# A two-layer hybrid diffusion step on one core: adaLN rows turned behind all sums, prompt tokens two k-tiles at a time, own buffers for the prompt's rotary results, last weights split later

## The chip, the cores and the metric

The kernel runs on one core of one Trainium2 chip. The metric is the device time of one launch in microseconds (us); where several runs were made, their median. Engines are named as in the profile: PE is TensorE's matmul queue and PEld its weight loads, DVE is VectorE, ACT is ScalarE, POOL is GpSimd, SP is SyncE, which issues nearly all DMAs of this kernel. Each engine works through its own queue strictly in order, so an instruction that waits holds up everything behind it on that engine.

## The reference

One step of a hybrid diffusion transformer with D = 1024 and two layers, over 1024 latent tokens ("sample") and 256 prompt tokens. Layer 0 has two head groups, a windowed attention with 16 heads and a bidirectional mLSTM with 4 heads; layer 1 is multi-head latent attention (MLA, 16 heads). Cut to what the change touches:

```python
def _adaln(cond, w, b):
    m = jax.nn.silu(cond) @ w + b                       # shift, scale, gate: 3 x 1024 columns
    shift, scale, gate = jnp.split(m[:, None, :], 3, axis=-1)
...
for l in range(DEPTH):
    sh_p, sc_p, gt_p = _adaln(c_ctx[None, :], w_mod[l], b_mod[l])
    sh_s, sc_s, gt_s = _adaln(c, w_mod[l], b_mod[l])
    hp = _rmsnorm(yp, norm_g[l]) * (1.0 + sc_p) + sh_p
    hs = _rmsnorm(ys, norm_g[l]) * (1.0 + sc_s) + sh_s
    ...                                                 # the mixer of the layer
    yp = yp + gt_p * out_p
    ys = ys + gt_s * out_s

def _mlstm_chunkwise(q, k, v, li, lf, C0, n0, m0):      # per head, chunk by chunk
    b = jnp.cumsum(lfc, axis=-1)                        # forget gates summed
    m_new = jnp.maximum(b_last + m, jnp.max(log_w, axis=-1))   # a running maximum
    w_s = jnp.exp(log_w - m_new[..., None])             # weights of the tokens
    ...

def _mixer_c(h, w_in, q_norm, w_qb, kv_norm, w_kvb, w_out, ctx, pos):
    qa, kva, kr, z = jnp.split(h @ w_in, C_SPLITS, axis=-1)
    q = (_rmsnorm(qa, q_norm) @ w_qb).reshape(B, T, C_HEADS, C_NOPE + C_ROPE)
    q_nope, q_rope = q[..., :C_NOPE], q[..., C_NOPE:]
    c_kv = _rmsnorm(kva, kv_norm)
    if ctx is not None:                                 # latent tokens only: rotary positions
        q_rope = _axial_rope(q_rope, rows, cols)
    k = jnp.concatenate([k_nope, jnp.broadcast_to(keys_kr, ...)], axis=-1)
    attn = _blocked_attn(qf, k, v, None, (C_NOPE + C_ROPE) ** -0.5)
    out = (attn * jax.nn.silu(z)) @ w_out
```

All is float32. The outputs are both token sets after the last norm, and the new caches and states.

## The kernel before, in words

**Products.** Each float32 product is three matmuls: a matrix is split into a rounded high part and the low rest, and high·high, high·low and low·high are summed in PSUM. A split is two instructions: ACT casts the high part (names that end in `h`: `wh`, `h1Th`, `cph`), then DVE or POOL subtracts it (`wl`, `h1Tl`, `cpl`). Tokens lie in three chunks, `CHUNKS`: 512 and 512 latent tokens and the 256 of the prompt.

**Order.** A first stage is written out by hand. Then comes a stage in which a scheduler puts the instructions of every engine in order (projections of layer 0, the mLSTM gates, the adaLN sums); a long hand-ordered middle (mLSTM and windowed attention); and again a scheduled rest: out projection, norm, layer 1's projections, latents and rotary parts, the MLA in seven `pair` stages with other work as filling, the output weights and the output. The scheduler keeps data dependences and orders by its own estimates, so one edit can shift the order of instructions far from it.

**PSUM.** In the first scheduled stage the 8 banks of PSUM are 6 for products (`S`) and 2 for transposes (`T`, from `psT`). A transpose writes a bank, and the bank is free once DVE or ACT has read it.

**adaLN sums** (`mod_sums`, lines 497 to 557). For six blocks of 512 columns, eight weight tiles `mw` (8 buffers) are loaded and summed by matmuls with the conditioning as stationary operand; ACT halves the sum into a tile `mrow1` (L512, `columns`). For scale and shift of layer 1 the tile must be turned to one column per token feature: `turned` transposes it on PE into a `T` bank, and DVE adds the bias (L522) and for scales multiplies by the norm's gain (L524). `mod_sums` is a generator, eight steps a block; a block's `turned` runs in the third step of the next one.

**The mLSTM's gates** (`gates`). Gate rows of 36 x 1280 are transposed in (`GI`, `GF`), scanned on DVE (L1579, L1580, L1586), combined (L1608 `LF`, L1609 `LI`, L1617 `rst`), exponentiated by ACT, and three of them go back by ten 36-row transposes each: `LI` into `cv`, `rst` into `cws`, `gM` into `cem`, each through one `T` bank that DVE copies out (L1642). `weave` alternates the steps of `gates` with shares of the projections of other blocks. DVE also has the mLSTM's convolution in its queue at that time (L1680, L1681, L1687, waiting for ACT's L1683).

**Layer 1's input** (`hT_chunk`, L785 and L786). Per k-tile of 128 features: transposes into a `T` bank, DVE scales and shifts into `hT_t`, ACT casts `h1Th`, DVE or POOL subtracts `h1Tl`. With the prompt a tile is 128 x 256.

**Rotary parts** (`k_rope`, `q_rope`, `rope_out`, `split_to`). The rotary part of keys and queries is split and stored to DRAM. The prompt's part has no rotation but goes through the same two-buffer tiles, `so_h` (ACT's cast, L867) and `rp_t` (the subtraction, L868); a buffer is free once its store has been read out by the DMA.

**Output weights** (`weights_out`, L2250 the cast `w`). Sixteen half tiles of `w_out` are loaded and each is split some steps behind its load, while the last MLA pair runs; `late` holds splits not yet issued, at most one between steps 6 and 11. In a pair, ACT also casts the transposed probabilities (`cph`, L2548), which PE needs for `V`.

## Time and profile before

| | us |
|---|---|
| median of 3 runs | 2566.37 (2564.22 to 2566.87) |
| the profiled execution | 2561.93 |
| its span in the profile | 2560.1 |
| PE busy in it | 2515.9 |
| DVE, ACT, POOL busy | 1699.3, 1437.2, 1128.9 |

The profile is one execution. Its own time is 1.8 us above its span. A row of the timeline gives the start, the length, engine and line, operation, tile out<-in, the shapes, and in square brackets how long the engine had been idle just before and what it waited for. A row of the windows gives the window, its length, busy time and number of instructions of PE, PEld, DVE, ACT and POOL, then the clock granted to PE as a share of full speed, the DMA share and GB/s. Lines are those of the kernel before; the end of a matmul is modelled, and neighbouring matmuls overlap, so that the distance of two starts, and not a row's length, is what one costs.

### The profile page before, as it was taken

The page shows a single profiled execution, that of the slowest core. Times are in us where ns is not written, and L with a number is a line of the kernel's source. Part 1 is how long each engine was busy: PE and PEld are TensorE (multiplying, and loading weights), DVE is VectorE, ACT ScalarE, POOL GpSimd, SP SyncE. Part 2 cuts the span into 40 slices and gives each one's busy share as a digit, 9 for nine tenths or more (in the row PEclk, how much of TensorE's full clock was granted, in tenths as well). Part 3 has the DMA queues.
Part 4 walks back from the last instruction along what each step waited for, and adds up shares of the span by engine and source line. Part 5 has one row for each costly group of instructions (what it writes and reads, how often), then busy time and mean ns, then how long its engine had stood idle before and what let it go on. Part 6 is the DMA issues. An engine that isn't in the chain of part 4 may idle for free.

```text
span 2560.1 us, 48511 instructions
## 1 busy us (share of the span) xinstructions
PE 2515.9 (98%) x16354; PEld 2246.2 (88%) x16354; DVE 1699.3 (66%) x4004; ACT 1437.2 (56%) x3665; POOL 1128.9 (44%) x1512
## 2 busy tenths in 40 slices
PE   8999999999999999999999999999999999999998
PEld 6998998998998888878888777898899989999887
DVE  6643656756657575687777456436888888888754
ACT  6423534535534432577666433134888888888842
POOL 6222333333324344366555543145455545555832
PEclk9999999999999999999999999999999999999999
DMA  7665575566667564455443554433211101111334
GB/s 265 214 178 177 156 222 184 170 202 190 188 205 222 181 216 151 118 171 164 128 133 94 173 159 162 124 82 114 63 35 30 39 29 41 32 31 29 123 98 134
DMA packets 339098, 347.52 MB, mean 136 GB/s; under 512 B 36425, under 2 KB 281854, under 8 KB 338594
## 3 DMA queue, kind: packets, MB, share of 16 engines
q1 hardware_dynamic: 338850, 344.43, 44.0%
q8 instruction: 130, 2.13, 0.3%
q14 instruction: 118, 0.97, 0.1%
HBM read 233.82 MB, written 110.50 MB: 134 GB/s over the span
## 4 chain that ended last, share of the span: by engine, by line
PE 83%; DVE 3%; issue 2%; ACT 2%; DMA 2%; POOL 1%; SPq 1%; POOLq 0%; DVEq 0%; ACTq 0%
PE mm L120 34%; PE S L120 28%; PE V L120 8%; PE T L124 7%; PE mm L124 2%; PE D L120 2%; SPq L155 1%; PE T L120 1%; DMA y<-w 0%; POOL w L1117 0%; DMA att_q<-ql 0%; DMA o_a<-aT 0%; ACT att_ph L1394 0%; DVE att_pl L1395 0%; POOL att_p L1383 0%
## 5 line engine op out<-in xcount | busy, mean ns | idle before, releaser
L583 POOL TENSOR_TENSOR wl<-wf,wh 128x256 fp32r<-128x256 f32 (+2 forms) x272 | 222.5, 843 | 484.3 <-ACT wh L582 396.4
L120 PE MATMUL mm<-hTh,wh 128*128 128x512 f32 (+1 forms) x912 | 329.2, 361 | 0.9 <-DVE scr L868 0.9
L120 PE MATMUL mm<-hTh,wl 128*128 128x512 f32 (+1 forms) x912 | 324.7, 356 | 0.0
L120 PE MATMUL mm<-hTl,wh 128*128 128x512 f32 (+1 forms) x912 | 324.1, 355 | 0.0
L120 PE MATMUL S<-cK,cQ 96*128 96x512 f32 (+3 forms) x1248 | 297.4, 363 | 0.8 <-ACT cPa L2501 0.7
L2549 DVE TENSOR_TENSOR cpl<-T,cph 128x512 fp32r<-128x512 f32 x336 | 228.7, 685 | 44.9 <-ACT cph L2548 41.7
L120 PEld LDWEIGHTS S<-cK,cQ 96*128 96x128 f32 (+1 forms) x1248 | 193.1, 189 | 22.3 <-ACT cPa L2501 2.7
L2548 ACT CAST cph<-T 128x512 fp32r<-128x512 f32 x336 | 192.4, 590 | 30.4 <-PE T L124 21.4
L120 PEld LDWEIGHTS mm<-hTh,wl 128*128 128x128 f32 x912 | 171.4, 188 | 26.9
L120 PEld LDWEIGHTS mm<-hTh,wh 128*128 128x128 f32 x912 | 171.5, 188 | 23.5 <-DVE scr L868 1.1
L120 PEld LDWEIGHTS mm<-hTl,wh 128*128 128x128 f32 x912 | 171.7, 188 | 23.2
L2499 DVE TENSOR_REDUCE cmx<-S 128x1 f32<-128x512 f32 x256 | 173.1, 682 | 18.2 <-PE S L120 17.1
L1395 DVE TENSOR_TENSOR att_pl<-mm,att_ph 128x512 fp32r<-128x512 f32 x168 | 116.0, 690 | 46.2 <-ACT att_ph L1394 44.0
L2480 POOL TENSOR_SCALAR cPa<-cPa,cst 128x512 f32<-128x512 f32 x128 | 98.4, 769 | 108.9 <-DVE cst L2477 92.0
L1394 ACT CAST att_ph<-mm 128x512 fp32r<-128x512 f32 x168 | 97.9, 582 | 76.0 <-PE mm L124 74.2
L120 PE MATMUL mm<-wh,hTh 128*128 128x256 f32 x480 | 135.5, 282 | 0.0
L120 PE MATMUL mm<-wl,hTh 128*128 128x256 f32 x480 | 134.9, 281 | 0.0
L120 PE MATMUL mm<-wh,hTl 128*128 128x256 f32 x480 | 134.5, 280 | 0.0
L582 ACT CAST wh<-wf 128x256 fp32r<-128x256 f32 (+2 forms) x272 | 96.4, 409 | 60.9 <-DMA wf<-in_w_in_c 28.8
L1383 POOL TENSOR_SCALAR att_p<-att_p,att_den 128x640 f32<-128x640 f32 (+1 forms) x128 | 97.5, 775 | 74.1 <-DVE att_p L1364 43.4
L1375 ACT ACTIVATE att_p<-att_p,att_nm 128x641 f32<-128x641 f32 (+1 forms) x128 | 103.4, 808 | 42.3 <-DVE att_nm L1369 35.4
L120 PE MATMUL V<-cph,cV 128*128 128x256 f32 x440 | 117.8, 288 | 1.3 <-ACT cph L2548 1.3
(489 smaller groups left out, 7908.7 us busy)
## 6 DMA issues: line engine op xcount, KB each, us to landing
wf<-in_w_in_ab SPq DMA_DIRECT2D x120, 256.0 KB
in<-in SPq DMA_DIRECT2D x40, 514.0 KB
in<-in SPq DMA_DIRECT2D x32, 386.0 KB
mw<-in_w_mod SPq DMA_DIRECT2D x48, 256.0 KB
in<-scr SPq DMA_DIRECT2D x40, 258.0 KB
o_x<-y SPq DMA_DIRECT2D x20, 512.0 KB
xin<-in_k_wmod SPq DMA_DIRECT2D x16, 512.0 KB
in<-cx SPq DMA_DIRECT2D x32, 256.0 KB
```

The lines of the kernel that those rows point to most:

```text
L120: return self.nc.tensor.matmul(out, lhsT, rhs, start=start, stop=stop)
L124: self.nc.tensor.transpose(out, in_, self.ident[:p, :p])
L582: K.nc.scalar.copy(wh, wf[:, k])
L583: K.nc.gpsimd.tensor_sub(wl, wf[:, k], wh.bitcast(F32))
L1375: self.A.K.nc.scalar.activation(pv, pv, AF.Exp, bias=nm[:, i], scale=-1.0, accum_out=den[:, i])
L1383: nc.gpsimd.tensor_scalar(pv, pv, den[:, i:i + 1], 1.0, ALU.mult, ALU.mult)
L1394: K.nc.scalar.copy(ph, self.T)
L1395: K.nc.vector.tensor_sub(pl, self.T, ph.bitcast(F32))
L2480: nc.gpsimd.tensor_scalar(pv, pv, wt[:, c:c + 1], rd, ALU.mult, ALU.mult)
L2499: nc.vector.tensor_reduce(mx[:, b, c:c + 1], S, AX.X, ALU.max, negate=True)
L2548: nc.scalar.copy(ph, T_)
L2549: nc.vector.tensor_sub(pl, T_, ph.bitcast(F32))
```

## The change

Five edits:

1. `mod_sums`: the halved sums stay in SBUF (`mrow1` gets 4 buffers instead of 2) in a list `waiting`; all four are transposed together into one `T` bank after the last sum, and the adds (after the change L524, L526) follow there.
2. `gates` has one more `yield`, before `cws`, and is woven in 6 steps instead of 5: `LI` goes out one step, `rst` and `gM` another.
3. `hT_chunk`: for the prompt a step takes two k-tiles of 256 columns in one bank; cast and subtraction work on 512 columns. Four casts and four subtractions instead of eight of each; which ones are on POOL changes with it.
4. `rope_out`: the prompt's rotary results get a pool `cu3` of their own with five buffers each for the high and the low part (`pr_h`, `pr_l`) in place of `so_h` and `rp_t`; the subtraction is on DVE. `k_rope` of the second latent chunk moves its additions from POOL to DVE.
5. `weights_out`: at most three pending splits in steps 6 to 12, one in step 13, instead of one in steps 6 to 11.

```diff
     def columns(ps, f):
-        rows = K.t(p, [128, 128], F32, "mrow1", 2)
+        rows = K.t(p, [128, 128], F32, "mrow1", 4)
         nc.scalar.mul(rows, ps[:, 0:128], 0.5)
-        return partial(turned, rows, f)
+        waiting.append((rows, f))
-    def turned(rows, f):
+    def turned():
         pc = K.psT()
-        K.tr(pc[:, 0:128], rows)
...
+        for i, (rows, f) in enumerate(waiting):
+            K.tr(pc[:, i * 128:(i + 1) * 128], rows)
+        for i, (rows, f) in enumerate(waiting):
...
+            nc.vector.tensor_add(dst, src, bc(bcol, 8 * a))
+            if a:
+                nc.vector.tensor_mul(dst, dst, bc(K.gcol, 8))
...
-            if i == 2 and late:
-                late = late()
...
-    if late:
-        late()
+    turned()
...
-    weave(gates(K, gp, gtp, gt), 5, dense.stream(2, 0.8), 20)
+    weave(gates(K, gp, gtp, gt), 6, dense.stream(2, 0.8), 20)
...
     for nm, src in (("cv", v), ("cws", ws), ("cem", M)):
         col = pp.tile([128, NT, 36], F32, tag=nm, name=nm)
+        if nm == "cws":
+            yield
         ps = K.psT()
...
-    for k in range(KD):
+    n = 512 // N
+    for j in range(KD // n):
+        ks = slice(j * n, (j + 1) * n)
...
+        hh, hl = [h[ci][:, ks].rearrange("p k t -> p (k t)") for h in (K.hTh, K.hTl)]
+        nc.scalar.copy(hh, t)
+        (nc.gpsimd if (j % 3 == 2 if n == 1 else j % 2) else nc.vector).tensor_sub(hl, t, hh.bitcast(F32))
...
+    elif not K.cu3:
+        split_to(K, K.cu2, ps, P, N, None, dh, dl, l=K.t(K.cu2, [128, 512], F32, "rp_t", 2))
     else:
-        split_to(K, K.cu2, ps, P, N, None, dh, dl, l=K.t(K.cu2, [128, 512], F32, "rp_t", 2))
+        h, l = [K.t(K.cu3, [128, 256], F32R, n, 5)[0:P, 0:N] for n in ("pr_h", "pr_l")]
+        K.nc.scalar.copy(h, ps[0:P, 0:N])
+        K.nc.vector.tensor_sub(l, ps[0:P, 0:N], h.bitcast(F32))
+        K.dma(dh, h)
+        K.dma(dl, l)
...
-            while len(late) > (1 if 6 <= i < 12 else 0):
+            while len(late) > (3 if 6 <= i < 13 else 1 if i == 13 else 0):
```

**On PE, in the stage of the gates.** Before (`mrow` tiles are turned in single transposes further up; `S<-wh,hTh` are projection matmuls):

```order
L120 MATMUL S_1931<-wh_1479,hTh_126 128x256
L120 MATMUL S_1931<-wl_1480,hTh_126 128x256
L120 MATMUL S_1931<-wh_1479,hTl_127 128x256
L124 MATMUL T_2130<-ident,LI 128x36 x10
L124 MATMUL T_2143<-ident,rst 128x36 x10
L120 MATMUL S_1956<-wh_1467,hTh_128 128x256
```

After:

```order
L120 MATMUL S_2010<-wh_1461,hTl_129 128x256
L124 MATMUL T_2044<-ident,LI 128x36 x10
L120 MATMUL S_1900<-wh_1467,hTh_126 128x256
...
L120 MATMUL S_1950<-wl_1480,hTh_128 128x256
L120 MATMUL S_1950<-wh_1479,hTl_129 128x256
L124 MATMUL T_2171<-ident,rst 128x36 x10
L124 MATMUL T_2184<-ident,gM 128x36 x10
L120 MATMUL S_2010<-wh_1467,hTh_128 128x256
```

`LI` stood directly ahead of `rst`, at place 850 of PE's queue; it now stands at place 799, with 72 projection matmuls between it and `rst`, which has moved from place 851 to 872; `gM` follows `rst` at once (before, it had 22 matmuls ahead of it, at place 874).

**On DVE, in the same stage**, between the scans and the additions that make `LI`. Before:

```order
L1586 SCALAR_TENSOR_TENSOR gM<-LF,m_1731,LI 4x1024 x2
L1664 COPY scr_1689<-S_1696 128x1
L1681 SCALAR_TENSOR_TENSOR cx_1808<-scr_1689,cw,cx_1808 128x512
L522 TENSOR_TENSOR B_1141<-T_1791,bcol_242_1137 128x4x2
L1680 SCALAR_TENSOR_TENSOR cx_1817<-scr_1804,cw,cx_1817 128x512
L1579 SCALAR_TENSOR_TENSOR gB<-rst,LF 4x1280
...
L1586 SCALAR_TENSOR_TENSOR gM<-LF,LI 4x256 x2
L1681 SCALAR_TENSOR_TENSOR cx_1817<-scr_1804,cw,cx_1817 128x512
L1687 SCALAR_TENSOR_TENSOR cx_1808<-scr_1812,cx_1808 128x512
```

After:

```order
L1590 SCALAR_TENSOR_TENSOR gM<-LF,m_1711,LI 4x1024 x2
L1583 SCALAR_TENSOR_TENSOR gB<-rst,LF 4x1280
L1584 SCALAR_TENSOR_TENSOR gB<-rst,LF 4x1280
L1590 SCALAR_TENSOR_TENSOR gM<-LF,LI 4x256 x2
L1670 COPY scr_1686<-S_1765 128x1
L1603 COPY bl<-gB 4x10
L1686 SCALAR_TENSOR_TENSOR cx_1811<-scr_1798,cw,cx_1811 128x512
L1604 COPY bl<-gB 4x10
```

The scans now follow one another; two L1681 and one L1687 of the convolution stand behind the additions that make `LI` (after the change they are L1687 and L1693), and the adaLN add L522 has left the stage.

**On PE, where the MLA begins**: behind the key transposes of the prompt (`u`), the query products `mm<-cq` of pair 0 and the key products `S<-hh`. Before:

```order
L120 MATMUL S_22448<-hh_4659_22058,wkl_22318 128x512
L124 MATMUL T_22341<-ident,u_22198 128x128
L124 MATMUL T_22336<-ident,u_22257 128x128
L124 MATMUL T_22341<-ident,u_22257 128x128
L120 MATMUL mm_22778<-cq_20199,wqh_22313 128x512
L120 MATMUL mm_22778<-cq_20200,wqh_22313 128x512
```

After:

```order
L120 MATMUL S_22433<-hh_4648_22039,wkl_22299 128x512
L124 MATMUL T_22325<-ident,u_22179 128x128
L124 MATMUL T_22320<-ident,u_22238 128x128
L124 MATMUL T_22325<-ident,u_22238 128x128
L120 MATMUL S_22444<-hh_4648_22039,wkh_22298 128x512
...
L120 MATMUL S_22500<-wvh_22302,hl_4649_22040 128x256
L120 MATMUL mm_22763<-cq_20180,wqh_22294 128x512
```

The first `mm<-cq` has moved from directly behind the transposes to 48 instructions behind them; key and value products stand there now.

**On ACT, beside the last pair**, the casts of the output weights (`w`) among the casts `cph`. Before:

```order
L2474 ACTIVATE cst_31792<-cmx_31661,cst_31792 128x3
L2250 CAST w_31695<-w_31693 128x512
L2250 CAST w_31695<-w_31720 128x512
L2548 CAST cph_31649<-T_31644 128x512
L2548 CAST cph_31675<-T_31670 128x512
...
L2548 CAST cph_31710<-T_31705 128x512
L2250 CAST w_31757<-w_31755 128x512
```

After (the same lines are L2489, L2265 and L2563):

```order
L2489 ACTIVATE cst_31773<-cmx_31646,cst_31773 128x3
L2265 CAST w_31680<-w_31678 128x512
L2265 CAST w_31680<-w_31705 128x512
L2563 CAST cph_31634<-T_31629 128x512
L2563 CAST cph_31660<-T_31655 128x512
...
L2563 CAST cph_31695<-T_31690 128x512
L2265 CAST w_31742<-w_31740 128x512
```

The first two casts stand between the same instructions as before.

## The prediction

> **What bounds the kernel now.** I read the page's head first, then the waits of PE, then the windows around the stages that the change touches.

> ```profile
> span 2560.1 us, 48511 instructions
> PE 2515.9 (98%) x16354; PEld 2246.2 (88%) x16354; DVE 1699.3 (66%) x4004; ACT 1437.2 (56%) x3665; POOL 1128.9 (44%) x1512
> PE 83%; DVE 3%; issue 2%; ACT 2%; DMA 2%; POOL 1%; SPq 1%; POOLq 0%; DVEq 0%; ACTq 0%
> ```

> PE is busy for 98% of the span, and the chain that ended last runs 83% through it. No other engine is near. The change leaves the number of matmul rows alone, so it can gain only in two ways: out of the 44.2 us in which PE stood idle (2560.1 − 2515.9), or where PE ran at a lower clock. The waits of PE say where idle time lies that the edits can reach:

> ```profile
> PE T L124 <- DVE A L522: 2.7, 1, 2.7
> PE mm L120 <- DVE rp_t L868: 2.4, 1, 2.4
> PE V L120 <- ACT cph L2548: 1.3, 1, 1.3
> PE S L120 <- ACT h1Th L785: 0.3, 1, 0.3
> PE S L120 <- POOL h1Tl L786: 0.3, 1, 0.3
> PE S L120 <- DVE sz_th L893: 0.3, 1, 0.3
> ```

> Each row is total, times, longest. These six, 7.3 us together, belong to edits 1 and 2, 4, 5 and 3 in this order. The first has a second price, which the windows show (length, then busy of PE, PEld, DVE, ACT, POOL, then PE's granted clock):

> ```profile
> 147.50:150.20 2.70, 0.01 (x1) 0.01 (x1) 1.58 (x9) 2.18 (x5) 0.00 (x0) 0.90 0.97 222
> 150.20:151.40 1.20, 1.18 (x11) 1.13 (x11) 0.84 (x5) 0.65 (x2) 0.00 (x0) 0.50 0.89 205
> 151.40:154.00 2.60, 2.60 (x13) 2.60 (x13) 1.75 (x7) 0.37 (x1) 0.00 (x0) 0.50 0.99 357
> 154.00:157.00 3.00, 3.00 (x22) 2.78 (x21) 0.00 (x0) 0.00 (x0) 0.00 (x0) 0.59 0.45 153
> ```

> After the gap PE is granted half its clock until nearly 157.

> **Edits 1 and 2, the gates.** The rows of PE and DVE around the gap:

> ```profile
> 146.70 0.81 PE L124 MATMUL T<-ident,LI 36*128 36x36 f32 x10
> 150.22 1.25 PE L124 MATMUL T<-ident,rst 36*128 36x36 f32 x10 [2.71 <-DVE A L522]
> 147.88 1.27 ACT L1618 ACTIVATE rst<-rst 36x1280 f32<-36x1280 f32 x1
> 149.49 0.42 DVE L1687 SCALAR_TENSOR_TENSOR cx<-scr,cx 128x256 f32<-128x256 f32 x1 [1.09 <-ACT scr L1683]
> 149.91 0.16 DVE L522 TENSOR_TENSOR A<-T,bcol 128x8 f32<-128x8 f32 x1
> ```

> The transposes of `rst` need a `T` bank. `LI` holds one; the other holds an adaLN row that L522 must read, and L522 is queued on DVE behind a convolution step that itself waits 1.09 for ACT. The data alone, `rst` exponentiated at 147.88 + 1.27 = 149.15, would have been late too, so both halves are needed: edit 1 takes the bank away from the adaLN row, edit 2 parts `LI` from `rst`. To price this I need the cost of a projection matmul and DVE's road to `LI`:

> ```profile
> 140.11 0.28 PE L120 MATMUL S<-wh,hTl 128*128 128x256 f32 x1
> 142.93 0.28 PE L120 MATMUL S<-wh,hTl 128*128 128x256 f32 x1
> 122.10 4.70 DVE L1586 TENSOR_TENSOR_SCAN gM<-LF,m,LI 4x1024 f32<-4x1024 f32 x2 [1.00 <-ACT LF L1567]
> 127.03 0.85 DVE L1681 SCALAR_TENSOR_TENSOR cx<-scr,cw,cx 128x512 f32<-128x512 f32 x1
> 137.70 1.04 DVE L1681 SCALAR_TENSOR_TENSOR cx<-scr,cw,cx 128x512 f32<-128x512 f32 x1
> 138.67 1.23 DVE L1687 SCALAR_TENSOR_TENSOR cx<-scr,cx 128x512 f32<-128x512 f32 x1
> 142.00 1.48 DVE L1609 TENSOR_TENSOR LI<-LI,gB 36x1280 f32<-36x1280 f32 x1
> ```

> The first two rows are 24 matmuls apart: (142.93 − 140.11) / 24 = 0.1175 us each.

> When `LI` is wanted: 51 places earlier, about 51 × 0.1175 = 6.0, so at 146.70 − 6.0 = 140.7. When it is ready: before at 142.00 + 1.48 = 143.48; two L1681, one L1687 and an L522 leave the road, 0.85 + 1.04 + 1.23 + 0.16 = 3.28, so 140.2, and up to the 1.00 that the scan waited for its input can go as well, since its transposes stand earlier too: 139.2 to 140.2. The slack is 0.5 to 1.5, thin. When `rst` is wanted: 140.7 + 0.8 for `LI` + 72 × 0.1175 = 8.5, thus 150.0. When it is ready: its road behind `LI` was 149.15 − 143.48 = 5.67; of the three operations pushed behind `LI`, 3.12, all may fall into it: 140.2 + 5.67 + 3.12 = 149.0. The slack is 1.0. The `LI` bank is needed for `gM` at 150.8, and its copy stands behind the last convolution step, whose end before was 149.49 + 0.42 = 149.9 and which has lost none of the work ahead of it but L522: slack 0.9.

> So I take the gap as gone, 2.7, and with it the low clock: 1.20 × 0.50 + 2.60 × 0.50 + 3.00 × 0.41 = 3.1. Together **5.8**. The bound above adds 2.70 × 0.10 = 0.3 for the 0.90 of the first window: 6.1. For the bound below, the thin slacks may each turn into a wait, the dearest being 1.0 at `LI`, and a queue on SP is passed:

> ```profile
> 153.05 0.32 SPq L155 DMA_DIRECT2D w0row<-dl  x1
> 156.92 0.80 SPq L155 DMA_DIRECT2D w0b<-w0row  x2
> ```

> `w0b` waits for `w0row` to land, 156.92 − 153.05 = 3.9 behind it. Two weight tiles `mw` of the next adaLN sum now stand behind `w0b`, and PE, running 5.8 ahead, reaches that sum sooner. I put nothing for it, and at most 1.5, less than half that row distance. Below: 5.8 − 1.0 − 1.5 = 3.3.

> [...]

> The added `yield` moves no data. The four transposes at the end of the sums replace four single ones, and the adds on DVE are the same six; the columns are read only by layer 1's input, over 1,300 us later, so lateness there costs nothing.

> **Edit 3, the prompt's 512 columns.** The forms of the tile (min, median, max ns):

> ```profile
> L782 DVE TENSOR_SCALAR hT_t<-T,A,B x24: 534/802/811, 1510.8 to 1579.7; 128x512 f32<-128x512 f32 x16, 128x256 f32<-128x256 f32 x8
> L785 ACT CAST h1Th<-hT_t x24: 405/620/626, 1511.7 to 1580.3; 128x512 fp32r<-128x512 f32 x16, 128x256 fp32r<-128x256 f32 x8
> L786 DVE TENSOR_TENSOR h1Tl<-hT_t,h1Th x18: 424/680/987, 1513.8 to 1580.7; 128x512 fp32r<-128x512 f32 x12, 128x256 fp32r<-128x256 f32 x6
> L786 POOL TENSOR_TENSOR h1Tl<-hT_t,h1Th x6: 722/1288/1300, 1516.5 to 1578.8; 128x512 fp32r<-128x512 f32 x4, 128x256 fp32r<-128x256 f32 x2
> ```

> The minimum is the 256 form, the median the 512 form. DVE: 6 × 0.42 = 2.5 of subtractions become 2 × 0.68 = 1.4, since two of four go to POOL; ACT: 8 × 0.405 = 3.2 become 4 × 0.62 = 2.5. DVE, which was the busy one here, gets 1.1 back, and the three waits of 0.3 (one each on ACT, POOL and DVE) hang on that supply. Against it, the last pair's subtraction is now one of 1.29 on POOL where the last one was 0.42 on DVE, 0.87 later. I take **0.7** of the 0.9; above 0.9, below 0.9 − 0.87 − 0.4 ≈ −0.4, if the last subtraction is waited for in full and a cast of 0.62 instead of 0.405 comes on top twice.

> **Edit 4, the rotary buffers.** Where the 2.4 lies:

> ```profile
> 1778.97 0.71 PE L120 MATMUL mm<-cq,wqh 128*128 128x512 f32 x2 [2.43 <-DVE rp_t L868]
> 1780.04 0.68 ACT L867 CAST so_h<-S 128x256 fp32r<-128x256 f32 x2 [1.12 <-DMA ckr<-so_h]
> 1782.25 0.84 ACT L867 CAST so_h<-S 128x256 fp32r<-128x256 f32 x2 [1.52 <-DMA cqr<-so_h]
> 1776.00:1779.00 3.00, 0.57 (x5) 0.31 (x3) 1.92 (x5) 2.65 (x6) 2.70 (x3) 1.00 0.54 185
> ```

> ACT waits 1.12 and 1.52 for stores to free `so_h`, and PE 2.43 for the banks behind these splits. With five buffers each these waits of ACT go, POOL (2.70 of 3.00 busy) loses the subtraction, and PE has 48 key and value products to do before the first `mm<-cq`. I take the whole **2.4**. That is also the bound above. Below: 1.3, if what ACT no longer waits for at 1780.04 is all that counts (1.12, and 0.2). This gap left the clock at 1.00, so it has no second price.

> **Edit 5, the weights.**

> ```profile
> 2384.00:2400.00 16.00, 14.08 (x93) 11.98 (x93) 11.82 (x28) 13.88 (x36) 14.18 (x19) 1.00 0.86 271
> 2387.35 0.62 ACT L2250 CAST w<-w 128x512 fp32r<-128x512 f32 x1 [1.02 <-DMA w<-in_w_out_c]
> 2388.73 0.62 ACT L2250 CAST w<-w 128x512 fp32r<-128x512 f32 x1 [0.76 <-DMA w<-in_w_out_c]
> 2389.25 1.06 ACT L2548 CAST cph<-T 128x512 fp32r<-128x512 f32 x2
> ```

> PE's 1.3 for `cph` is ACT's 1.02 + 0.76 on two loads with the `cph` casts queued behind. If the casts stood later, 1.92 of PE's idle here (16.00 − 14.08) could go. But in the changed order these two casts stand between the same instructions, and some of the following ones come earlier; only loads are issued further ahead. So **0**; above 1.9, below −1.2, two more casts (0.62 each) ahead of `cph` while ACT is 87% busy.

> **The rest.** The scheduler also reshuffles the MLA pairs:

> ```profile
> 1808.00:2384.00 576.00, 573.16 (x3999) 524.41 (x3998) 497.84 (x1155) 492.77 (x1364) 313.28 (x543) 1.00 0.12 35
> ```

> Only 2.84 of 576 are idle; **0**, ±1.5 (half of it).

> **Sum.** 5.8 + 0.7 + 2.4 + 0 + 0 = 8.9. On the profiled execution 2561.93 − 8.9 = 2553.0; that execution is 4.4 below the median of the runs, so for the median 2566.37 − 8.9 = **2557.5**. All upper bounds give 6.1 + 0.9 + 2.4 + 1.9 + 1.5 = 12.8, thus 2553.6; all lower ones 3.3 − 0.4 + 1.3 − 1.2 − 1.5 = 1.5, thus 2564.9.

> **Rivals.**

> *The weights do gain.* The loads, issued further ahead, have landed when the two casts come, and 1.9 is added: 2555.6. For it: 1.02 and 0.76 are waits for loads. Against it: the DMA share is 0.86 in that window, and the first two loads are no earlier.

> *The clock is lost anyway.* `LI` comes late by 1.0, the ten small transposes and that gap lie together again, and half clock follows: 1.0 + 3.1 come back, 2557.5 + 4.1 = 2561.6. For it: the slack of 0.5. Against it: the 2.43 gap at 1776 stayed at 1.00, so 1.0 is short.

> *The gain is handed back.* PE, 5.8 early, meets loads that are not, and waits somewhere before 200 us for them: 2557.5 + 5.8 = 2563.3. For it: the DMA share of 0.97 to 0.99 at 147.5 and 151.4. Against it: 0.45 directly behind.

> *Slower: one bank for `mm` in the pairs.* In the new order a query or key product of each pair comes to PE before its one `mm` bank has been read, and costs what that cost once, 2.43, in each of the seven pairs: 17.0, thus 2574.5. It decides from four pairs on (9.7 against 8.9), and from six on (14.6) it is slower by more than 0.2%. For it: that 2.43 is of this kind, a product waiting for a bank behind a DVE subtraction. Against it: 2.84 idle in all pairs before.

> **How the numbers follow.** This kernel's runs lie within 0.1% of each other; about 0.2%, 5.1 us, can be told from no change, so faster means under 2561.2. Chances: the forecast 0.55, the weights 0.13, the lost clock 0.12, the gain handed back 0.12, slower 0.08. Faster gets 0.53 of the first, the 0.13, and 0.06 of the lost clock's cases: 0.72. Within gets 0.02, 0.06 and 0.12: 0.20. Slower 0.08. The range goes from 2552.5, a little below all upper bounds, since the median itself moves by 1 us between runs, to 2564.5, which takes in the lost clock and the gain handed back and leaves out the slow rival.

> **What would show it.** In the profile after: no wait of PE at `rst` and the granted clock at 1.00 between 140 and 160 (edits 1 and 2; a wait at `LI` with clock at 0.50 behind it is the second rival); the `h1Th`/`h1Tl` waits under 0.2; no `so_h` wait on ACT near the MLA's beginning, and `mm<-cq` without idle ahead; the `cph` wait of 1.3 still there. Wrong would make it: PE idle over 1.0 in total at new places before 200 us, or over 8 between the MLA's beginning and the last pair.

## The result, and the profile after

The changed kernel takes 2552.76 us (median of 4 runs, 2551.34 to 2554.30) against 2566.47 for the kernel before beside it: ratio 0.9948, 95% interval 0.9936 to 0.9960. Timed again in a later group (experiment 5) it takes 2550.96 against 2565.51, ratio 0.9939 (0.9925 to 0.9952). So it is faster by 13.7 to 14.6 us. Forecast were 2557.5, 8.9 us faster, and a range of 2552.5 to 2564.5. The first time lies at its lower edge, and the later one 1.5 below it.

The two profiled executions differ by 10.4 us, less than the medians do. The head of the page after, and three of PE's waits:

```profile
span 2549.7 us, 48524 instructions
PE 2510.6 (98%) x16354; PEld 2242.6 (88%) x16354; DVE 1698.3 (67%) x4002; ACT 1438.1 (56%) x3661; POOL 1129.8 (44%) x1510
...
PE V L120 <- ACT cph L2563: 1.3, 1, 1.3
PE mm L120 <- DVE cQ L2135: 0.8, 1, 0.8
PE S L120 <- POOL h1Tl L790: 0.4, 1, 0.4
```

PE's idle time fell from 44.2 to 39.1 us (2549.7 − 2510.6), and its busy time by 5.3 though it does the same 16354 matmuls: part of the gain is clock. The waits on L522 and on `rp_t` are gone, the one on `cph` is where it was. PE's first `mm<-cq` has no idle time ahead, but a later product there waits 0.8 for DVE (`cQ`, above).

Where the lead is won can be read from landmarks, the first and last start of PE's matmuls with a tile that marks a stage. Before:

```profile
L120 PE MATMUL S<-mw,condP x384: 272/273/297, 91.3 to 200.2; 128*32 128x128 f32 x192
L124 PE MATMUL T<-ident,xs x80: 270/272/314, 1486.4 to 1577.6; 128*128 128x128 f32 x80
L124 PE MATMUL T<-ident,u x60: 270/272/274, 1698.7 to 1776.3; 128*128 128x128 f32 x50, 128*32 128x128 f32 x10
L120 PE MATMUL V<-cph,hh x116: 277/281/391, 1812.5 to 2383.8; 128*128 128x256 f32 x116
L120 PE MATMUL V<-cph,cV x440: 276/280/384, 1821.1 to 2501.8; 128*128 128x256 f32 x147
```

After:

```profile
L120 PE MATMUL S<-mw,condP x384: 272/273/297, 92.0 to 194.6; 128*32 128x128 f32 x192
L124 PE MATMUL T<-ident,xs x80: 270/272/328, 1480.9 to 1570.5; 128*128 128x128 f32 x80
L124 PE MATMUL T<-ident,u x60: 270/273/274, 1689.8 to 1767.4; 128*128 128x128 f32 x50, 128*32 128x128 f32 x10
L120 PE MATMUL V<-cph,hh x116: 277/281/387, 1798.7 to 2372.9; 128*128 128x256 f32 x116
L120 PE MATMUL V<-cph,cV x440: 276/280/387, 1806.5 to 2491.3; 128*128 128x256 f32 x147
```

The last adaLN sum (`mw`) starts 5.6 us earlier, the first transpose of layer 1's input (`xs`) still 5.5, the last of `u` 8.9, the last `V<-cph,hh` 10.9, the last `V<-cph,cV` 10.5. So edits 1 and 2 won 5.6 (forecast 5.8), the stage from `xs` to `u` with edit 3 won 3.4 (0.7), the MLA with edit 4 2.0 (2.4), and the last pair with edit 5 lost 0.4 (0).

In the stage of the gates, the windows of before and then of after:

```profile
140.00:160.00 20.00, 17.26 (x132) 16.49 (x131) 13.06 (x37) 6.61 (x13) 0.00 (x0) 0.83 0.67 178
```

```profile
140.00:160.00 20.00, 20.00 (x227) 19.31 (x226) 12.46 (x36) 8.01 (x18) 2.28 (x2) 1.00 0.77 225
...
141.00 0.81 PE L124 MATMUL T<-ident,LI 36*128 36x36 f32 x10
...
L124 PE MATMUL T<-ident,rst x10: 226/227/250, 150.4 to 151.0; 36*128 36x36 f32 x10
```

No idle time, clock 1.00. `LI` is at 141.00 (worked out: 140.7), `rst` at 150.4 (150.0).

### The profile page after: what moved, and what is told of

Its sections match the earlier page's. It is cut to its first block, busy times and chain, and to the rows that moved or that the text cites. A ratio compares the mean times of both kernels' runs of the same rounds, so it can differ in the third digit from the quotient of the medians.

```text
span 2549.7 us, 48524 instructions
## 1 busy us (share of the span) xinstructions
PE 2510.6 (98%) x16354; PEld 2242.6 (88%) x16354; DVE 1698.3 (67%) x4002; ACT 1438.1 (56%) x3661; POOL 1129.8 (44%) x1510
## 4 chain that ended last, share of the span: by engine, by line
PE 88%; DVE 3%; DMA 3%; ACT 2%; issue 2%; SPq 1%; POOL 1%; POOLq 0%; ACTq 0%; DVEq 0%
PE mm L120 35%; PE S L120 33%; PE V L120 8%; PE T L124 7%; PE mm L124 2%; PE D L120 2%; SPq L155 1%; PE T L120 1%; DMA xin<-in_k_wmod 0%; DMA att_q<-ql 0%; DVE cpl L2564 0%; DVE att_pl L1399 0%; DMA o_a<-aT 0%; DVE cmx L2514 0%; ACT att_ph L1398 0%
## 5 line engine op out<-in xcount | busy, mean ns | idle before, releaser
L120 PE MATMUL mm<-hTh,wh 128*128 128x512 f32 (+1 forms) x912 | 329.4, 361 | 0.9 <-DVE scr L872 0.9
L120 PE MATMUL mm<-hTh,wl 128*128 128x512 f32 (+1 forms) x912 | 324.9, 356 | 0.0
L120 PE MATMUL mm<-hTl,wh 128*128 128x512 f32 (+1 forms) x912 | 324.3, 356 | 0.0
L120 PE MATMUL S<-cK,cQ 96*128 96x512 f32 (+3 forms) x1248 | 300.3, 365 | 1.6 <-ACT cPb L2516 1.2
L2563 ACT CAST cph<-T 128x512 fp32r<-128x512 f32 x336 | 192.0, 589 | 39.9 <-PE T L124 26.9
L120 PEld LDWEIGHTS S<-cK,cQ 96*128 96x128 f32 (+1 forms) x1248 | 192.9, 189 | 23.1 <-ACT cPb L2516 3.1
L120 PEld LDWEIGHTS mm<-hTh,wl 128*128 128x128 f32 x912 | 171.5, 188 | 26.9
L120 PEld LDWEIGHTS mm<-hTh,wh 128*128 128x128 f32 x912 | 171.6, 188 | 23.5 <-DVE scr L872 1.1
L120 PEld LDWEIGHTS mm<-hTl,wh 128*128 128x128 f32 x912 | 171.8, 188 | 23.1
L2495 POOL TENSOR_SCALAR cPa<-cPa,cst 128x512 f32<-128x512 f32 x128 | 98.7, 771 | 117.6 <-DVE cst L2492 93.5
L120 PE MATMUL mm<-wh,hTh 128*128 128x256 f32 x480 | 135.5, 282 | 0.0
L120 PE MATMUL mm<-wl,hTh 128*128 128x256 f32 x480 | 135.0, 281 | 0.0
L120 PE MATMUL mm<-wh,hTl 128*128 128x256 f32 x480 | 134.6, 280 | 0.0
L120 PE MATMUL V<-cph,cV 128*128 128x256 f32 x440 | 118.3, 289 | 1.5 <-ACT cph L2563 1.3
```

Of the source, the lines that this page charges most:

```text
L120: return self.nc.tensor.matmul(out, lhsT, rhs, start=start, stop=stop)
L2495: nc.gpsimd.tensor_scalar(pv, pv, wt[:, c:c + 1], rd, ALU.mult, ALU.mult)
L2563: nc.scalar.copy(ph, T_)
```

## The experiments

Twelve runs, each timed in five rounds beside the kernel before. The time of one kernel scatters by some 2 us from execution to execution, so three measures stand side by side: the ratio of the runs, the stages in the one profiled execution, and the mean over a kernel's runs of the granted clock.

| | median us | ratio to before, 95% | mean clock (runs) | start to last `mw` | `xs` to `u` | `u` to `cph,hh` | `cph,hh` to `cph,cV` |
|---|---|---|---|---|---|---|---|
| before, first profile | 2565.5 | 1 | 0.9973 (63) | 200.2 | 289.9 | 607.5 | 118.0 |
| 11: before again | 2565.91 | 1.0003 (0.9994 to 1.0011) | 0.9972 (11) | 200.6 | 290.1 | 609.2 | 117.4 |
| changed, first profile | 2552.76 | 0.9948 (0.9936 to 0.9960) | 0.9993 (4) | 194.6 | 286.5 | 605.5 | 118.4 |
| 5: changed again | 2550.96 | 0.9939 (0.9925 to 0.9952) | 0.9990 (5) | 193.9 | 287.2 | 605.4 | 118.3 |
| 1: without edits 1, 2 | 2561.12 | 0.9982 (0.9974 to 0.9991) | 0.9975 (11) | 199.8 | 287.1 | 605.8 | 118.3 |
| 2: without edit 3 | 2554.55 | 0.9963 (0.9951 to 0.9975) | 0.9984 (5) | 194.8 | 288.5 | 605.4 | 118.6 |
| 3: without edit 4 | 2555.45 | 0.9967 (0.9955 to 0.9980) | 0.9980 (7) | 194.3 | 286.6 | 609.3 | 119.6 |
| 4: without edit 5 | 2553.89 | 0.9957 (0.9945 to 0.9968) | 0.9992 (5) | 194.8 | 287.2 | 605.4 | 117.3 |
| 6: edit 1 alone | 2560.54 | 0.9981 (0.9972 to 0.9990) | 0.9976 (11) | 198.0 | 288.2 | 608.4 | 121.0 |
| 7: edit 2 alone | 2565.80 | 1.0002 (0.9993 to 1.0011) | 0.9974 (11) | 199.0 | 289.9 | 609.0 | 118.4 |
| 8: weights 7, subtraction on DVE | 2550.88 | 0.9941 (0.9928 to 0.9953) | 0.9992 (5) | 193.9 | 286.4 | 605.5 | 118.3 |
| 9: edits 1, 2 alone | 2556.40 | 0.9967 (0.9955 to 0.9979) | 0.9988 (5) | 193.8 | 289.0 | 606.7 | 117.6 |
| 10: edit 4 alone | 2564.53 | 1.0001 (0.9992 to 1.0009) | 0.9977 (11) | 198.7 | 290.2 | 606.4 | 118.4 |
| 12: edits 1, 2, 4 | 2557.51 | 0.9969 (0.9957 to 0.9980) | 0.9986 (7) | 195.5 | 288.5 | 605.4 | 118.6 |

Medians and clocks in the first row are over the 63 runs of before in the three groups. The stage columns run from the last start of the one landmark to that of the other (from the first start for `xs`). What lies between the last `mw` and the first `xs` is not in the table. There PE does the same matmuls in the same order before, after and in experiments 9 and 12 (apart from the four turned rows at its start); it took 1286.2 us in the first trace of before, 1286.3 in that of the changed kernel, and 1285.2 to 1290.8 over all fourteen traces. So single traces can differ by some us without any edit.

**1. The changed kernel without edits 1 and 2.**

```diff
-    weave(gates(K, gp, gtp, gt), 6, dense.stream(2, 0.8), 20)
+    weave(gates(K, gp, gtp, gt), 5, dense.stream(2, 0.8), 20)
```

and `mod_sums` and `gates` as before.

> The changed kernel with edits 1 and 2 undone (adaLN rows turned one by one, gates woven in 5 steps); edits 3 to 5 stay. Theory (the gap at rst and the half clock behind it are worth what the prediction says, and nothing later gives the lead back): PE idle of 2.7 us at rst and a granted clock of 0.5 until about 157 are back, PE reaches the last adaLN sum 5.6 us later than in the changed kernel, and the whole time is 5.6 longer, about 2558.4, ratio to before 0.997. Rival (a lead won at 160 us is partly handed back later, or the other edits need it): under 2 us longer, about 2554, ratio 0.995.

The wait of 2.7 on L522 and the half clock are back (granted 0.60 from 148 to 152 and 0.54 from 152 to 156), and the stage takes 199.8. The theory of the stage holds; the rival, a gain handed back, falls. The whole time is longer than expected: 2561.1 rather than 2558.4, and 8.4 to 10.2 longer than the changed kernel, where the theory had 5.6.

**2. Without edit 3** (`hT_chunk` as before).

> The changed kernel with edit 3 undone (prompt tokens one k-tile at a time). Theory of the prediction (its worth is the three listed waits): 0.7 to 0.9 us longer, about 2553.6. Rival from the trace of after (its worth is larger, because ACT and DVE also reach the next block's weight splits sooner): 2.5 to 3.4 us longer, about 2556; the waits for h1Th, h1Tl, sz_th and those for wh and wl 10 us behind them come back together.

The waits at the prompt's units are there again:

```profile
PE S L120 <- ACT h1Th L784: 0.3, 1, 0.3
PE S L120 <- POOL h1Tl L785: 0.3, 1, 0.3
PE S L120 <- DVE sz_th L892: 0.3, 1, 0.3
```

`xs` to `u` takes 288.5. In the eight traces without the edit it takes 288.2 to 290.2 (mean 289.3), in the six with it 286.4 to 287.2 (mean 286.8): 2.5 us, so the rival's size is right. (One of the eight, the second trace of before, has a stretch of half clock in this stage.) Its reason is not: the waits for `wh` and `wl` did not come back here, and they are missing in the second trace of the kernel before as well. Why the three waits of 0.3 cost more than 0.9 the starts of before show:

```profile
1580.15 0.28 PE L120 MATMUL S<-h1Th,wl 128*128 128x256 f32 x1
1580.75 0.39 PE L120 MATMUL S<-h1Th,wh 128*128 128x256 f32 x1 [0.32 <-ACT h1Th L785]
1581.21 0.39 PE L120 MATMUL S<-h1Tl,wh 128*128 128x256 f32 x1
```

Undisturbed, such matmuls start 0.12 apart (0.1175 in the rows of the prediction). Here the distances are 0.60 and 0.46, 0.82 us lost, of which the list shows 0.32: it counts only what lies beyond the modelled end of the matmul ahead (0.28 long), and nothing for the second distance. Summed in this way over the starts from 1578.9 to 1582.3, the three waits cost about 2.0. In the trace after, the wait of 0.4 for `h1Tl` costs about 0.6. That explains 1.4 of the 2.5; where the rest lies is not shown.

**3. Without edit 4** (`rope_out` and `k_rope` as before, no `cu3`).

> The changed kernel with edit 4 undone (prompt's rotary results in the two-buffer tiles). Theory: ACT waits for stores again at the beginning of the MLA, PE about 2 us in front of the first query product, time 2.0 to 2.4 longer, about 2555. Rival (the scheduler's new order, with key and value products ahead of the query products, hides it without own buffers): under 0.5 longer, and no PE wait over 1 us there.

ACT waits for the stores of `so_h` again (1.09 and 1.52), PE waits 1.98 before a query product again (for `cK`, at 1794.9) and 1.45 before the first one, and `u` to `cph,hh` takes 609.3 against 605.5: 3.8 longer. Most of that is clock: the second stretch named below lasts 6.8 us, which is 3.4 us lost. The runs fall into two groups, four at 2553.5 to 2555.5 and three at 2560.8 to 2562.4, with clocks of 0.998 to 0.999 and of 0.996 to 0.998. The profiled one is of the second, and its clock was halved in three places (from 1231.2, 1794.4 and 2388.3), the last behind the `cph` wait of 1.2 in the last pair:

```profile
2386.00:2388.00 2.00, 0.72 (x3) 0.53 (x4) 1.09 (x2) 2.00 (x6) 1.53 (x2) 1.00 1.01 347
2388.00:2390.00 2.00, 2.00 (x11) 1.81 (x10) 0.90 (x2) 2.00 (x7) 2.00 (x4) 0.58 1.01 370
2390.00:2392.00 2.00, 2.00 (x12) 1.90 (x11) 1.34 (x2) 1.98 (x6) 2.00 (x4) 0.57 1.05 423
```

The same wait left the clock at 1.00 in the profiles of before and after. So the rival (order alone hides it) falls in the trace: PE waits over 1 us there. In the runs the median is 2.7 to 4.5 longer than the changed kernel's, where the theory had 2.0 to 2.4; the half clock in part of the executions was not in it.

**4. Without edit 5** (one pending split).

> The changed kernel with edit 5 undone (at most one pending split). Theory of the prediction (the first two casts stand where they stood, so the edit does nothing): time within 1 us of the changed kernel, 2552 to 2553.5, PE's wait for cph 1.2 to 1.4 in both. Rival (loads issued further ahead gain): 1 to 2 us longer, and the cph wait over 1.6.

The last column is 117.3, 1.1 less than with the edit, the `cph` wait 0.9. That wait is 1.3 in the first trace of the changed kernel and 0.6 in the second, so it scatters by as much. The time, 2553.89, is a little over the expected 2552 to 2553.5, but the interval overlaps that of the changed kernel. The traces show no gain from the edit; the rival's wait of over 1.6 did not come, but its 1 to 2 us are not excluded by the runs.

**5. The changed kernel again.**

> The changed kernel itself, unaltered, timed again in more rounds beside the runs of this group: its ratio to the kernel before should be 0.9948 within 0.001, about 13 us faster. If it is nearer to 0.996 (10.4 us, the difference of the two profiled executions), the larger first figure was scatter of the runs.

0.9939: the larger difference is the right one, and the first figure was not scatter. The profiled execution of before, 2561.93, is quicker than 72 of the 74 runs of that kernel timed in these groups, so that a forecast made on it rests on a lucky draw.

**6. Edit 1 alone.**

> The kernel before with edit 1 alone (adaLN rows turned behind all sums; gates woven in 5 steps as before). Theory of the prediction (both halves are needed: the bank by edit 1, the data of rst, late by 1.65 us in its own right, by edit 2): a gap of 1 to 2 us at rst remains, with or without the low clock behind it; 1 to 3 us faster than before. Rival (taking the add out of DVE's queue is enough for the scheduler to part LI from rst by itself, as its order of instructions has it): no gap, granted clock 1.00 from 140 to 160, 5 to 6 us faster than before, ratio 0.998.

```profile
146.15 0.81 PE L124 MATMUL T<-ident,LI 36*128 36x36 f32 x10
149.15 0.81 PE L124 MATMUL T<-ident,rst 36*128 36x36 f32 x10 [2.19 <-ACT rst L1617]
```

`LI` stays directly ahead of `rst`; the list of instructions that the rival went by was not this kernel's order on the chip. The bank is free, and the data are late: PE waits 2.19 for ACT, and `rst` starts at 149.15, the time worked out in the prediction from 147.88 + 1.27 (that it agrees to the last digit is luck). The clock was 0.88 from 148 to 152 and 0.69 from 152 to 156, and the stage won 2.2 us of 5.6. The prediction's theory holds. The ratio says 5 us, more than the stage: the profiled execution has three stretches of half clock (from 151.0, 1775.8 and 2397.0), while the kernel before has one in its first trace and four in its second.

**7. Edit 2 alone.**

> The kernel before with edit 2 alone (the added yield and 6 steps; the adaLN rows still turned one by one). Theory of the prediction (both halves are needed): rst or gM waits for the bank that an adaLN row holds until its add on DVE, 1 us or more, and up to 3 us of low clock. Rival (parting LI from rst is enough): no wait over 0.3 us there, clock 1.00, 5 to 6 us faster than before, ratio 0.998.

```profile
148.88 0.33 PE L124 MATMUL T<-ident,mrow 128*128 128x128 f32 x1 [2.15 <-ACT mrow L512]
```

A single adaLN row now stands between `LI` (142.9) and `rst` (154.8), and PE waits for it; the clock stayed at 1.00 there in this trace. This wait is another one than the theory had (for the row itself, not for the bank behind it). The theory's wait is in the trace too, but earlier: at 107.39 the transposes of the gate rows (`GI`) wait 2.17 for a bank that an adaLN row holds until its L522 on DVE. The stage wins 1.2 us, and edit 2 alone gives nothing in the time, 1.0002.

**8. More pending weights, last subtraction on DVE.**

```diff
-        (nc.gpsimd if (j % 3 == 2 if n == 1 else j % 2) else nc.vector).tensor_sub(hl, t, hh.bitcast(F32))
+        (nc.gpsimd if (j % 3 == 2 if n == 1 else j == 1) else nc.vector).tensor_sub(hl, t, hh.bitcast(F32))
...
-            while len(late) > (3 if 6 <= i < 13 else 1 if i == 13 else 0):
+            while len(late) > (7 if 6 <= i < 14 else 0):
```

> The changed kernel with two small alterations: up to seven pending weight splits in steps 6 to 13 (the first two casts then stand behind three casts of cph in ACT's queue), and of the prompt's four subtractions only the second on POOL, so that the last is on DVE. Theory (PE's 1.3 us for cph is the two casts that wait for their loads ahead of it; the 0.4 us for h1Tl is POOL's 1.29 us subtraction): both waits go, 1.5 to 2.0 us faster than the changed kernel. Rival (the wait has other grounds, or casts pushed back collide with later cph casts): cph wait stays over 1 us or a new one of that size comes within 15 us; time within 1 us of the changed kernel.

Both waits are gone, 1.7 us, and nothing is won: 2550.88 against 2550.96, last column 118.3 as before. What PE waits for in the last pair now:

```profile
PE V L120 <- DVE cst L2488: 1.3, 3, 0.5
PE T L124 <- DVE cpl L2564: 0.5, 2, 0.3
```

The 1.3 came back as three waits on DVE's `cst` within the same 15 us (0.2 in the changed kernel; the row of `cpl` is the same there). The rival holds. The second trace of the changed kernel says the same: its `cph` wait is only 0.6, and its last column is 118.3 too. The two waits' own causes were as the theory said. This kernel cannot be told from the changed one.

**9. Edits 1 and 2 alone.**

> The kernel before with edits 1 and 2 only. Theory (each long wait of PE costs its own length and, in part of the executions, a stretch of half clock behind it; edits 1 and 2 take away the one that does so in nearly every execution): 5.6 us less up to the last adaLN sum in the trace, 5 to 7 us less in the median, and the mean granted clock over the runs up from 0.9973 by 0.001 to 0.0015, not to the 0.9991 of the changed kernel, since the wait of 2.4 us in front of the MLA is still there. Rival (the whole clock gain hangs on edits 1 and 2): clock 0.999 and 8 us or more.

The stage takes 193.8 and the clock rises to 0.9988; 2556.40 against 2565.63 is 9.2 us. The clock's rise of 0.0015 is at the upper edge of what the theory had and close to the rival's 0.999; the gain in the runs is rather the rival's (8 us or more), though the interval, 5.4 to 11.5 us, takes in the theory's 5 to 7 in part. What the runs gain beyond the stage's 6.4 is thus not decided.

**10. Edit 4 alone.**

> The kernel before with edit 4 only (own buffers for the prompt's rotary results). Theory of the prediction (the 2.4 us gap and no second price): 2 to 3 us faster, mean granted clock as before, 0.9973. Rival (the gap halves the clock in part of the executions, as it does in three other traces): 3 to 5 us faster and a mean clock of 0.9977 to 0.998.

1.0001. Neither holds: the 2.4 wait is gone from the list, `u` to `cph,hh` is 1.1 shorter than in the first trace of before, and the time is the same. The 95% interval ends at 2.1 us faster and so leaves out the 2.4. Its worth seems to depend on what else is changed (experiment 3); that stays open.

**11. The kernel before again**, nothing altered.

> The kernel before, unaltered, for a second profiled execution of it. Ratio 1. Theory (the first profiled execution, 4 us under the median, was one in which half clock followed only the gap at rst): its time is nearer to the median, and besides 148 to 157 us there is at least one more stretch of half clock, likeliest behind the 2.4 us gap at 1776 or the 1.3 us one at 2389. Rival (the scatter of the runs lies in DMA waits of the middle): clock as in the first trace, and 2 to 4 us more of idle PE between 200 and 1400 us.

Its windows at the prompt's units and at the beginning of the MLA:

```profile
1582.00:1584.00 2.00, 1.34 (x6) 0.88 (x6) 1.57 (x3) 1.42 (x3) 0.00 (x0) 0.86 0.00 0
1584.00:1586.00 2.00, 2.00 (x11) 2.00 (x11) 2.00 (x6) 1.15 (x3) 1.08 (x2) 0.50 0.72 233
1586.00:1588.00 2.00, 2.00 (x15) 2.00 (x15) 2.00 (x4) 1.15 (x3) 1.46 (x2) 0.78 0.80 218
...
1778.00:1780.00 2.00, 0.42 (x4) 0.18 (x2) 1.26 (x3) 1.87 (x5) 1.71 (x2) 1.00 0.56 171
1780.00:1782.00 2.00, 1.15 (x4) 1.00 (x5) 1.31 (x3) 0.86 (x3) 1.26 (x1) 0.86 0.49 151
1782.00:1784.00 2.00, 2.00 (x6) 1.54 (x6) 0.76 (x2) 0.61 (x2) 0.00 (x0) 0.50 0.57 173
```

And the first trace at the same place:

```profile
1780.00:1784.00 4.00, 4.00 (x19) 3.28 (x18) 1.33 (x4) 2.04 (x6) 0.00 (x0) 1.00 0.64 180
```

The wait for `rp_t` is 2.43 in both traces. Half clock follows the gap at `rst` in both; in the second also from 1146.6 (0.64 from 1146 to 1148, 0.51 from 1148 to 1150), behind the prompt's three short waits at 1582, and behind the 2.43 wait. The theory holds.

**12. Edits 1, 2 and 4.**

> The changed kernel with edits 3 and 5 undone, that is edits 1, 2 and 4. Theory (edit 5 is worth nothing, edit 3 about 2 us): 2 to 3 us longer than the changed kernel, ratio to before 0.995 to 0.9955, mean clock 0.9985 or more. Rival (edits 3 and 5 carry a good part of what the prediction missed): ratio 0.9965 or more.

0.9969, which lies in the rival's range: in the runs, edits 3 and 5 bring some 5 to 7 us on top. The profiled execution is also 6.0 longer than that of the changed kernel, but only 2.0 of it lies in the stage of edit 3. 3.0 lies between the last `mw` and the first `xs`, where PE's matmuls are the same, and where it waits 4.7 instead of 2.6 for the loads of `att_q`. That part of the difference is scatter.

## Why the prediction was right, and where not

The direction, the place of the main gain and its mechanism were right. The time fell 13.7 to 14.6 instead of 8.9. Three steps were off, all to the same side; how much of the difference each of them carries is shown only in part. That the time came out at the edge of the range owes something to luck, since most of what was missed stood in none of its bounds.

**Edits 1 and 2, 5.8: right in the traces, and more in the runs.** 5.6 in the first pair of traces; over the traces with both edits the stage takes 194.5 on average (eight), without both 199.8 (four). `LI` and `rst` came within 0.4 of the times worked out. The slack at `LI` was 1.3 (ready at 139.67, started at 141.00; forecast 0.5 to 1.5), that at `rst` 3.1 (ready at 147.29; forecast 1.0), and the sum behind `w0b` did not wait. That both halves are needed is shown by the traces of experiments 6 and 7: 198.0 and 199.0 against 193.8 with both. The windows that the prediction prices hold 1.20 + 2.60 + 3.00 × 0.41 / 0.50 = 6.3 us at half clock, and 6.8 with what lies in the first of them; its price of 3.1, and 3.4 with the upper bound, is worked out rightly. In the runs the pair is worth 9.2 (experiment 9) and 8.4 to 10.2 (experiment 1); what adds to the 5.6 there no trace shows.

**Edit 3, 0.7: mis-sized.** It is worth 2.5 in the stage. The step that failed is the price: the three listed waits of 0.3 were taken for the whole loss, when two starts alone had lost 0.82, and the three waits about 2.0. The bound above, 0.9, came from the same list and was no bound. The worry about the last subtraction on POOL was right and small: a wait of 0.4, where under 0.2 was given as the sign.

**Edit 4, 2.4: the term nearly fits its trace, the step "no second price" is wrong.** In the first pair the stage won 2.0: PE's waits in the 40 us from the last transposes of `u` on add up to 3.5 before and to 1.6 after. Of the six traces with that wait of 2.0 to 2.4, four have half clock behind it (experiments 3, 6, 7, 11) and two do not (the first of before, and 9). `u` to `cph,hh` takes 609.0 on average with it and 607.1 without, against 605.6 in the eight traces with the edit. So the wait costs 1.5, and 1.9 more in part of the executions. I had read what happened in one execution as a property of the place; what tells the executions apart is not shown. In the runs of edit 4 alone none of this is seen, which the traces don't explain.

**Edit 5, 0: right as far as the traces go.** The order of the casts on ACT was read rightly; the rows after:

```profile
2375.82 0.62 ACT L2265 CAST w<-w 128x512 fp32r<-128x512 f32 x1 [0.46 <-DMA w<-in_w_out_c]
2377.74 0.62 ACT L2265 CAST w<-w 128x512 fp32r<-128x512 f32 x1 [1.30 <-DMA w<-in_w_out_c]
```

0.46 + 1.30 = 1.76 against 1.78 before.

**The base.** The sum was made on an execution that was 3.6 us quicker than the median of all runs since, and set on the median as it was. That assumes that what makes other executions slower stays. The prediction also took the runs to lie within 0.1% of each other, from three of them; the 63 since lie between 2561.4 and 2570.4. What makes them slower did not stay: the mean clock rose from 0.9973 (63 runs of before) to 0.9991 (9 runs of the changed kernel). Worked out from these, 0.0018 × 2556 is 4.6 us of clock, where the prediction had 3.1. The clock's gain is thus more than the one place I had priced. The other 8.7 of the 13.3 between the means (2565.45 and 2552.1) has no trace of its own: in the first pair of traces, 3.4 of 10.4 was clock, and PE's idle time fell by 5.1.

The rivals: the weights gained nothing in the traces, the clock was not lost at `LI`, nothing was handed back by 200 us (the lead was 5.6 there and 5.5 at 1486), and PE's idle time in the pairs did not grow (2.84 of 576 before, 1.68 of 570 after). One sign that would have spoken against the prediction came by its letter: in the first 100 us PE waits 1.5 longer in the trace after, mostly for the input tiles `xin`. The unaltered kernel does so too in its second trace (1.2 longer), so this is scatter.

Open: why the runs gain more than the stages of the traces show, for edits 1 and 2 as for edits 3 and 5, and why edit 4 gains nothing alone. With five to eleven runs per kernel the intervals leave 2 to 3 us on each.

## What to carry to other kernels

A list of waits gives less than a stall costs where short matmuls are pipelined: price it by the distance of the starts (0.32 in the list against 0.82 in the starts, experiment 2). A wait of PE may have a second price in one execution and none in the next (2.43 in both traces of before, with the clock at 0.50 behind it in the second and at 1.00 in the first), so read the clock over all runs of a kernel, not in one trace, before calling a gap free. And where a cast stands in front of a critical one, see first what the critical one waits for next: taking the first wait away may only show the second (experiment 8: the 1.3 for `cph` gone, 1.3 for `cst` in its place).

## What the runs showed of the hardware

These stretches have only two lengths here. Worked out from the clocks of narrow windows, fourteen of the eighteen last 3.41 us and four last 6.83, twice that; so one costs 1.7 or 3.4 us. The one in the first trace of before is one of the long ones, from 149.64 to 156.47; the one behind 1582 above is a short one, at half clock for 2.00 × 0.14 / 0.5 + 2.00 + 2.00 × 0.22 / 0.5 = 3.4 us. In the second trace of before they start at 149.86, 1146.55, 1583.46 and 1781.43. PE's idle time at these was 2.7 us in one wait, 0.86 and 0.72 in two, 0.37 and 0.66 in the two windows of 2.00 from 1580 on, and 2.43 in one wait: less than 2.8 us each time.

The length of a wait alone does not tell whether half clock follows. In the second trace of before the wait of 2.43 runs from 1778.42 to 1780.85, and half clock begins at 1781.43. In the first it is as long, from 1776.54 to 1778.97, and the clock is at 1.00 from 1776 to 1788. Behind the same wait half clock follows in experiment 6 (from 1775.8), while in experiment 9 the clock is at 1.00 from 1768 to 1778. In experiment 3 half clock begins at 1794.4, when PE had been idle for 1.45. What tells these cases apart is not shown.
